# A decoder layer on one core: 66 buffers instead of 51, an RWKV norm without a root, joined softmax steps, and x divided by its rms from piece 20 instead of 35

## The chip, the cores and the metric

The kernel runs on one core of one Trainium2 chip. Five engines work on their own queues: TensorE (PE, with its weight loads shown apart as PEld), VectorE (DVE), ScalarE (ACT), GpSimd (POOL) and SyncE (SP), which here issues nearly all DMAs. The metric is the device time of one execution in microseconds; of several executions the median counts. A profile is one more execution with the profiler on; its span runs from the first to the last instruction of the program.

## The reference

One layer over 256 tokens of width 2048, in float32. Two groups of heads read the same normed x through one projection of 7832 columns:

```python
hn = rms_norm(h, pre_norm_g); proj = hn @ w_in            # 2048 -> 7832
q, kv6, gates, z_a, feat_b, z_b = split(proj)
# group A, 8 query heads on 2 key heads: compressed blocks, selected blocks, window
o = g0 * softmax(q kc + bias) vc + g1 * softmax(q ks + bias) vs + g2 * softmax(q kw + bias) vw
# group B, 16 heads of 64: RWKV-7
kk = k * k_k;  kk = kk / max(sqrt(sum(kk * kk)), 1e-12)   # per head
state = state * w_t + (state a_t) b_t^T + v_t k_t^T;  y = state r_t   # a = -kk, b = kk * a
mix = concat([o * silu(z_a), (groupnorm(y) + bonus) * silu(z_b)])
h = h + rms_norm(mix @ w_out, post_norm_g)
```

## The kernel before

**Pieces.** The projection is worked off in pieces of 128 output columns, in the order of the list `FM`: piece 0 for the two LoRAs, 12 pieces of the first half of RWKV (k, r, v), 8 pieces of compressed, selected and window keys (13 to 20), 12 pieces of RWKV's second half, 8 of q, 16 of z; a token-major part stands after piece 36. Each piece runs over 16 blocks of 128 rows of x, in two half pieces of 8 (`half_piece`). To keep float32 precision every operand is split into a rounded high part and a low rest; a half piece loads one block of weights (512 KB, SP, L312, tile `rf`), ACT rounds it (L320, tile `hf`), DVE subtracts (L321, tile `lf`), and PE multiplies three times: high by high x, high by low x, low by high x. Several blocks are loaded and split ahead of PE. All matmuls come from one helper line, L169; transposes are L198.

**The two forms of a piece.** The high and low part of x lie side by side in `xs_` (tiles xs_75 and xs_76 in the rows below). Up to piece `N_SWITCH - 1` x is not yet divided by its rms, both products with the high weights go into the same 256 columns, and the evacuation multiplies by the reciprocal rms (`evacuate`, L614, one DVE instruction). From piece `N_SWITCH` on (`beside`) x has been divided, and one matmul of 512 columns does both products side by side; then the evacuation adds the two halves, an ACT copy (L616) and a DVE instruction (L617):

```python
if beside:
    mm(pt[:], H[:, k, :], xHL[kk_], start=kk_ == 0, stop=False)
else:
    mm(pt[:, :T], H[:, k, :], xH[kk_], start=kk_ == 0, stop=False)
    mm(pt[:, :T], H[:, k, :], xL[kk_], start=False, stop=False)
```

For the change of form `stage` fetches x a second time, 2 transfers of 1 MB (L524), into 2 times 8 buffers, and multiplies it (16 DVE instructions, L527); it starts 6 pieces ahead of the switch. `renewed` splits it anew into `xs_` (4 ACT copies L537, 4 DVE L538). So that PE has work meanwhile, the two pieces ahead of the switch and the two behind it are done first half by first half, then second half by second half.

**Other work.** RWKV's first half: per 128 columns (`block`, four of them) `k_norm` sums squares per head on PE, `k_rsqrt` takes the root on ACT and the reciprocal on DVE (L686) for two at a time, `rwkv_k` builds scaled keys, `rwkv_r` a masked product (L782). Then `solve` inverts 64 triangular blocks in a loop of 62 DVE instructions (L832, L834), with round trips through DRAM before (`us`, L819 and L825) and after (`zs`, `zt`, L841 to L859), and runs four chunks of the state. The second half does the same later. A group normalisation (L983 to L1002) ends each half. `compress` multiplies 8 blocks of 512 KB (`in_cw`, L1029), fetched by `fetch_cw` when at least 12 buffers are free. `nsa_head`, eight times, does logits, softmax and the weighted sum. Last comes the output projection in 4 groups of 512 columns (tiles `ho`, `lo`); its products with group A's mix (tiles mixA) come first for three groups, the ones with RWKV's mix (mixB) after.

**What sets the order.** The generators are stepped in lanes by a counter of PE time, and a scheduler of the framework with its own timing model then fixes each engine's instruction order at build time. On the chip every engine works off its queue in that order. Temporary storage is one arena of `UNITS` buffers of 1 KB per partition, handed out by `Pool.find`, which weighs how long a buffer has been free.

Of the kernel before, what the change touches and what calls it, by code (L numbers as in the profile page):

```python
# [16 lines left out]
P = 128  # L17
# [36 lines left out]

N_SWITCH = 35

# [5 lines left out]

UNITS = 51
NSMALL = 2912

NLAST = 4
# [15 lines left out]
class Pool:  # L82
# [8 lines left out]
    def find(self, k, step=1):  # L91
        best = None
        for a in range(0, len(self.busy) - k + 1, step):
            if not any(self.busy[a:a + k]):
                beside = (a > 0 and self.busy[a - 1]) + (a + k < len(self.busy) and self.busy[a + k])
                late = max(0.0, max(self.since[a:a + k]) - self.clock[0])
                key = (late, -beside if k < 3 else 0, a if k >= 3 else -a)
                if best is None or key < best[0]:
                    best = (key, a)
        return None if best is None else best[1]  # L100
# [34 lines left out]
def hybrid_block(ctx: ExitStack, tc: tile.TileContext, xT, xtok, wfm, wtm, wout, vecs, gpost, lora, table,  # L135
# [535 lines left out]
    def k_norm(A, i, m):  # L671
        sq = yield from sb()
        ACT.activation(sq[:], A.ks[i], AF.Square, scale=vcol(V_KK, m))
        sp = yield from bank()
        yield from head_sums(sp, sq)
        DVE.tensor_scalar(A.nrm[i], sp[:, :T], 1e-24, None, op0=ALU.max)
        sp.free(2.0)
        yield 0.5

    def k_rsqrt(A, i):  # L680
        nrm = A.pair[i // 2].ap.rearrange("p (a b t) -> p a b t", a=2, b=2)[:, 1]
        yield 1.5
        ACT.activation(nrm, nrm, AF.Sqrt)  # L683
# [20 lines left out]
    def rwkv_k(A, i, m):  # L704
# [3 lines left out]
        for a in range(2):  # L708
# [15 lines left out]
        pi = yield from sb()  # L724
        kk = yield from sb()
        st.prs = pr
# [5 lines left out]
        POOL.tensor_copy(A.PC[:, i, :], pr4[:, :, 63:64].rearrange("p c o -> p (c o)"))  # L732
        DVE.scalar_tensor_tensor(kk[:], k, vcol(V_KK, m), A.nrm[i], op0=ALU.mult, op1=ALU.mult)  # L733
        DVE.tensor_tensor(k, k, fk[:], op=ALU.mult)
# [5 lines left out]
        DVE.tensor_tensor(KB[:, :, 0:4:3, :], k.rearrange("p (a b t) -> p a b t", a=2, b=2), pi4, op=ALU.mult)  # L740
        kk4 = kk.ap.rearrange("p (c t) -> p c t", c=4)
        DVE.tensor_tensor(A.AR[:, i, :, 0, 1:64], kk4[:, :, 1:64], pr4[:, :, 0:63], op=ALU.mult)
        POOL.tensor_copy(A.AR[:, i, :, 0, 0:1], kk4[:, :, 0:1])  # L743
        yield 0.8
        DVE.tensor_tensor(ta[:], ta[:], kk[:], op=ALU.mult)
# [348 lines left out]
    def nsa_head(h, qts):  # L1094
# [52 lines left out]
        yield 1.0  # L1147
        for i in range(2):
            DVE.tensor_scalar(sm[:, i, :], sm[:, i, :], 1e-30, None, op0=ALU.max)
            DVE.reciprocal(sm[:, i, :], sm[:, i, :])  # L1150
            DVE.tensor_tensor(sm[:, i, :], sm[:, i, :], gate[:, i, h:24:8], op=ALU.mult)
            n = (7, 15)[i]
            src = lc[:, i, None, 0:n].to_broadcast([P, 2, n])
            hh_ = lcs[:, i, 0:64].rearrange("p (r n) -> p r n", r=2)[:, :, 0:n]
            DVE.tensor_scalar(hh_, src, sm[:, i, 0:1], None, op0=ALU.mult)
            DVE.scalar_tensor_tensor(lcs[:, i, 64:64 + n], lc[:, i, 0:n], sm[:, i, 0:1],
                                     lcs[:, i, 0:n].bitcast(F32), op0=ALU.mult, op1=ALU.subtract)
            for j in (1, 2):
                dst = parts[i][j][2]
                if i == 1:  # L1160
                    ACT.activation(dst, dst, AF.Copy, scale=sm[:, i, j:j + 1])
                else:
                    DVE.tensor_scalar(dst, dst, sm[:, i, j:j + 1], None, op0=ALU.mult)
            yield 1.2

# [91 lines left out]
    for j, (nm, i) in enumerate(FM):  # L1257
# [13 lines left out]
        elif nm == "k":  # L1271
# [235 lines left out]
```

## Time and profile before

| | |
|---|---|
| median of 3 executions | 559.15 us (558.38 to 561.14) |
| the profiled execution | 558.53 us, of which the span is 556.7 us |
| PE busy, PEld busy | 542.6 us (97%), 492.7 us (88%) |
| DVE, ACT, POOL busy | 434.2 us (78%), 319.5 us (57%), 54.9 us (10%) |
| granted TensorE clock | 0.998 |
| DMA | 102.02 MB, mean 183 GB/s |

A row of a group reads: line, engine, operation, output and inputs by the program's names, count, then busy time, mean duration of one in ns, and the idle time of the engine just before it with what ended it. A row of the timeline reads: start in us from the span's start, length of the run of like instructions, engine and line, what it is, count, and in brackets the idle time before it and its releaser. A busy PE is not a PE at its peak, since the ends of matmuls overlap; the distance between two starts is the better measure.

### The profile page before, as it was taken

The page shows a single profiled execution, that of the slowest core. Times are in us where ns is not written, and L with a number is a line of the kernel's source. Part 1 is how long each engine was busy: PE and PEld are TensorE (multiplying, and loading weights), DVE is VectorE, ACT ScalarE, POOL GpSimd, SP SyncE. Part 2 cuts the span into 40 slices and gives each one's busy share as a digit, 9 for nine tenths or more (in the row PEclk, how much of TensorE's full clock was granted, in tenths as well). Part 3 has the DMA queues.
Part 4 walks back from the last instruction along what each step waited for, and adds up shares of the span by engine and source line. Part 5 has one row for each costly group of instructions (what it writes and reads, how often), then busy time and mean ns, then how long its engine had stood idle before and what let it go on. Part 6 is the DMA issues. An engine that isn't in the chain of part 4 may idle for free.

```text
span 556.7 us, 11510 instructions
## 1 busy us (share of the span) xinstructions
PE 542.6 (97%) x4448; PEld 492.7 (88%) x4448; DVE 434.2 (78%) x910; ACT 319.5 (57%) x592; POOL 54.9 (10%) x93
## 2 busy tenths in 40 slices
PE   9999999998999999999999899999999999899995
PEld 8999999998999999988998788988888887688883
DVE  6888997984998976697799969997856675746654
ACT  6958854644436532545857858765665546455532
POOL 3101310420000000001305100100000000000000
PEclk9999999999999999999999999999999999999999
DMA  8957455477755576553346435445632466456624
GB/s 298 381 195 268 142 172 176 142 249 225 263 193 171 180 203 222 182 172 95 110 150 211 139 108 169 154 161 167 193 127 86 136 219 271 168 189 220 195 79 151
DMA packets 41170, 102.02 MB, mean 183 GB/s; under 512 B 14203, under 2 KB 16412, under 8 KB 40476
## 3 DMA queue, kind: packets, MB, share of 16 engines
q1 hardware_dynamic: 40828, 100.98, 55.1%
q8 instruction: 35, 0.57, 0.4%
q10 hardware_dynamic: 288, 0.31, 0.2%
q14 instruction: 19, 0.16, 0.1%
HBM read 96.03 MB, written 5.24 MB: 182 GB/s over the span
## 4 chain that ended last, share of the span: by engine, by line
PE 84%; DVE 6%; DMA 5%; ACT 2%; issue 1%; SPq 1%; DVEq 0%; ACTq 0%
PE banks L169 82%; DMA arena<-in_cw_dram 2%; PE banks L198 2%; DMA zs<-arena 1%; DMA xr<-in_xT_dram 1%; DMA us<-GR 1%; DMA arena<-zt 1%; DVE GR L782 1%; DVE arena L1002 0%; DVE arena L527 0%; DVE arena L834 0%; DVE arena L832 0%; ACT arena L1142 0%; ACT L987 0%; ACT L715 0%
## 5 line engine op out<-in xcount | busy, mean ns | idle before, releaser
L169 PE MATMUL banks<-arena 128*32 128x128 f32 (+3 forms) x470 | 29.5, 253 | 3.2 <-DMA arena<-in_cw_dram 1.8
L169 PEld LDWEIGHTS banks<-arena 128*32 128x32 f32 (+3 forms) x470 | 25.0, 136 | 7.2 <-DMA arena<-in_cw_dram 2.2
L832 DVE TENSOR_TENSOR arena<-arena 64x31 f32<-64x31 f32 (+15 forms) x62 | 20.4, 329 | 6.2 <-DMA arena<-us 5.6
L631 ACT ACTIVATE small<-small 128x256 f32<-128x256 f32 x25 | 12.3, 501 | 17.6 <-DVE small L614 17.6
L834 DVE TENSOR_TENSOR arena<-arena 64x31 f32<-64x31 f32 (+15 forms) x62 | 20.4, 330 | 0.7
L198 PE MATMUL banks<-small,arena 128*128 128x128 f32 x96 | 15.4, 277 | 1.8 <-DVE arena L989 0.7
L198 PEld LDWEIGHTS banks<-small,arena 128*128 128x128 f32 x96 | 11.1, 140 | 4.2 <-DVE arena L989 1.1
L686 DVE RECIPROCAL arena<-arena 128x256 f32<-128x256 f32 x8 | 13.6, 1730 | 1.3 <-ACT arena L683 1.3
L1142 ACT ACTIVATE arena<-arena,mx 128x128 f32<-128x128 f32 (+1 forms) x32 | 14.1, 443 | 0.0
L632 DVE SCALAR_TENSOR_TENSOR arena<-small 128x256 f32<-128x256 f32 x25 | 11.8, 477 | 2.0 <-ACT small L631 1.9
L719 POOL TENSOR_SCALAR arena<-arena,small 128x256 f32<-128x256 f32 x8 | 9.3, 1164 | 39.3 <-ACT arena L717 39.1
L1138 DVE CUSTOM_DVE_ANT_0 arena<-banks,arena 128x128 f32<-128x128 f32 (+1 forms) x32 | 10.0, 347 | 3.0 <-DMA zt<-arena 3.0
L614 DVE SCALAR_TENSOR_TENSOR small<-banks,small 128x256 f32<-128x256 f32 x29 | 11.9, 417 | 0.1
L169 PEld LDWEIGHTS banks<-VS,GR 128*64 128x64 f32 x256 | 9.6, 137 | 2.5 <-issue 1.4
L955 POOL MEMSET arena<- 64x256 f32 x12 | 3.7, 307 | 81.2 <-DVE lf__2469 L321 44.8
L782 DVE TENSOR_TENSOR GR<-banks,small 128x1024 f32<-128x1024 f32 x8 | 9.7, 1215 | 2.3 <-PE banks L169 2.2
L169 PE MATMUL banks<-VS,GR 128*64 128x64 f32 x256 | 11.4, 228 | 0.0
L743 POOL COPY AR<-arena 128x4 f32<-128x4 f32 x8 | 7.3, 909 | 34.9 <-DVE arena L733 34.9
L169 PE MATMUL banks<-AR,arena 64*128 64x128 f32 x128 | 10.0, 287 | 0.0
L716 POOL TENSOR_SCALAR arena<-arena 128x256 f32<-128x256 f32 x8 | 8.1, 1018 | 17.5 <-ACT arena L715 17.5
L527 DVE SCALAR_TENSOR_TENSOR arena<-arena,small 128x256 f32<-128x256 f32 x16 | 6.5, 479 | 4.3 <-DMA arena<-in_xT_dram 4.3
L169 PEld LDWEIGHTS banks<-AR,arena 64*128 64x128 f32 x128 | 8.1, 187 | 1.4 <-issue 0.3
(1166 smaller groups left out, 1802.4 us busy)
## 6 DMA issues: line engine op xcount, KB each, us to landing
arena<-in_cw_dram SPq DMA_DIRECT2D x8, 512.0 KB, 5.2
arena<-in_wfm_dram SPq DMA_DIRECT2D x4, 512.0 KB, 9.2
arena<-in_xT_dram SPq DMA_DIRECT2D x2, 1024.0 KB, 5.9
xres<-in_xtok_dram SPq DMA_DIRECT2D x2, 1024.0 KB, 5.7
out_dram<-y SPq DMA_DIRECT2D x7, 256.0 KB, 2.4
xr<-in_xT_dram SPq DMA_DIRECT2D x3, 512.0 KB, 7.2
bscr<-arena SPq DMA_DIRECT2D x1, 1536.0 KB, 5.9
arena<-bscr SPq DMA_DIRECT2D x8, 128.0 KB, 2.2
```

The lines of the kernel that those rows point to most:

```text
L169: last[0] = PE.matmul(o, lhsT, rhs, **kw)
L198: PE.transpose(out=o, in_=i, identity=idn)
L614: DVE.scalar_tensor_tensor(o, pt[:, :T], scale, rbc, op0=ALU.mult, op1=ALU.mult)
L631: ACT.activation(tm, f[:, 0:T], AF.Copy, scale=vcol(V_MU, c))
L632: DVE.scalar_tensor_tensor(o, f[:, 1:T + 1], omu[:, c:c + 1], tm, op0=ALU.mult, op1=ALU.add)
L686: pace(DVE.reciprocal(A.nrm[i + j], A.nrm[i + j]))
L719: POOL.tensor_scalar(fk[:], ta[:], ka2[:, m:m + 1], ka1[:, m:m + 1], op0=ALU.mult, op1=ALU.add)
L782: DVE.tensor_tensor(A.GR[:, i].rearrange("p h c t -> p (h c) t"), gp.ap.rearrange("p h (c t) -> p (h c) t", c=4), gmask[:, None, :].to_bro ...
L832: DVE.tensor_tensor(t_, U[:, 0:j, j:j + 1].to_broadcast([64, j, w]), Z[:, j:j + 1, j:32].to_broadcast([64, j, w]), op=ALU.mult)
L834: DVE.tensor_tensor(Z[:, 0:j, j:32], Z[:, 0:j, j:32], t_, op=ALU.add)
L1138: DVE.tensor_tensor_reduce(out=dst, in0=src, in1=bb, scale=1.0, scalar=-3.0e38, op0=ALU.add, op1=ALU.max, accum_out=mx[:, i, j:j + 1])
L1142: ACT.activation(dst, dst, AF.Exp, bias=mx[:, i, j:j + 1], accum_out=sm[:, i, j:j + 1])
```

## The change

Five things at once. The arena has 66 buffers instead of 51 (the room comes from a DMA scratch area set to 1 KB) and its choice adds `REST` = 40 us to the time after which a buffer counts as rested. RWKV's norm takes no root: since the product of two normed vectors is wanted, the reciprocal of the sum of squares is taken from PSUM at once and multiplied in later; `k_rsqrt` and its root on ACT go. The per-head steps after the softmax handle both row blocks with one instruction each. And `N_SWITCH` is 20 instead of 35.

```diff
-N_SWITCH = 35
+N_SWITCH = 20
-UNITS = 51
+UNITS = 66
+REST = 40.0
...
-                late = max(0.0, max(self.since[a:a + k]) - self.clock[0])
+                late = max(0.0, max(self.since[a:a + k]) + REST - self.clock[0])
...
-        DVE.tensor_scalar(A.nrm[i], sp[:, :T], 1e-24, None, op0=ALU.max)
-        sp.free(2.0)
+        DVE.reciprocal(A.nrm[i], sp[:, :T])
+        sp.free(3.0)
         yield 0.5
 
-    def k_rsqrt(A, i):
...
-        ACT.activation(nrm, nrm, AF.Sqrt)
-        yield 1.5
+    def k_ready(A, i):
         for j in range(2):
-            pace(DVE.reciprocal(A.nrm[i + j], A.nrm[i + j]))
+            yield 0.3
             A.normed[i + j] = True
-            yield 1.2
...
-        DVE.scalar_tensor_tensor(kk[:], k, vcol(V_KK, m), A.nrm[i], op0=ALU.mult, op1=ALU.mult)
+        DVE.scalar_tensor_tensor(A.AR[:, i, :, 0, 1:64], k4[:, :, 1:64], vcol(V_KK, m), pr4[:, :, 0:63], op0=ALU.mult,
+                                 op1=ALU.mult)
+        POOL.tensor_scalar(A.AR[:, i, :, 0, 0:1], k4[:, :, 0:1], vcol(V_KK, m), None, op0=ALU.mult)
+        DVE.scalar_tensor_tensor(ta[:], k, vcol(V_KK, m), ta[:], op0=ALU.mult, op1=ALU.mult)
...
-        DVE.tensor_tensor(A.AR[:, i, :, 0, 1:64], kk4[:, :, 1:64], pr4[:, :, 0:63], op=ALU.mult)
-        POOL.tensor_copy(A.AR[:, i, :, 0, 0:1], kk4[:, :, 0:1])
         yield 0.8
-        DVE.tensor_tensor(ta[:], ta[:], kk[:], op=ALU.mult)
+        DVE.scalar_tensor_tensor(ta[:], A.nrm[i], 1e24, ta[:], op0=ALU.min, op1=ALU.mult)
...
+        POOL.memset(lc, 0.0)
...
-        for i in range(2):
-            DVE.tensor_scalar(sm[:, i, :], sm[:, i, :], 1e-30, None, op0=ALU.max)
-            DVE.reciprocal(sm[:, i, :], sm[:, i, :])
-            DVE.tensor_tensor(sm[:, i, :], sm[:, i, :], gate[:, i, h:24:8], op=ALU.mult)
...
+        DVE.tensor_scalar(sm, sm, 1e-30, None, op0=ALU.max)
+        DVE.reciprocal(sm, sm)
+        DVE.tensor_tensor(sm, sm, gate[:, :, h:24:8], op=ALU.mult)
+        lgv = bass.AP(tensor=lg.tensor, offset=lg.offset, ap=[lg.ap[0], [384, 2], [1, 128]])
+        DVE.tensor_tensor(lgv, lgv, sm[:, 0, 1:3, None].to_broadcast([P, 2, P]), op=ALU.mult)
+        for j in (1, 2):
+            dst = parts[1][j][2]
+            ACT.activation(dst, dst, AF.Copy, scale=sm[:, 1, j:j + 1])
+        DVE.tensor_tensor(lc, lc, sm[:, :, 0:1].to_broadcast([P, 2, 16]), op=ALU.mult)
+        DVE.tensor_copy(lcs[:, :, 0:64].rearrange("p i (r n) -> p i r n", r=2)[:, :, :, 0:16],
+                        lc[:, :, None, :].to_broadcast([P, 2, 2, 16]))
+        DVE.tensor_tensor(lcs[:, :, 64:80], lc, lcs[:, :, 0:16].bitcast(F32), op=ALU.subtract)
+        yield 2.4
...
-                rw.append(k_rsqrt(A, i % 4 - 1))
+                rw.append(k_ready(A, i % 4 - 1))
...
-    nc = _bacc.Bacc("TRN2", target_bir_lowering=False, num_devices=1)
+    nc = _bacc.Bacc("TRN2", target_bir_lowering=False, num_devices=1, dynamic_dma_scratch_size=1024)
```

Since the scheduler fixes the order anew, it differs on every engine. Three places are shown; a row is line, operation, output and inputs, size, count, and lines of the changed kernel stand two or three off (L1029 is L1026 there, L321 is L323, L169 is L171, L198 is L200).

SP's queue around the compression weights (`in_cw`, for `compress`), before:

```order
L1035 DMA small<-in_cw_dram 128x256
L312 DMA rf__1420<-in_wfm_dram 128x1024
L312 DMA rf__1471<-in_wfm_dram 128x1024
L312 DMA rf__1518<-in_wfm_dram 128x1024
L312 DMA rf__1560<-in_wfm_dram 128x1024
L312 DMA rf__1603<-in_wfm_dram 128x1024
L1029 DMA arena<-in_cw_dram 128x1024
L312 DMA rf__1647<-in_wfm_dram 128x1024
L1029 DMA arena<-in_cw_dram 128x1024
L312 DMA rf__1684<-in_wfm_dram 128x1024
L312 DMA rf__1724<-in_wfm_dram 128x1024
L1029 DMA arena<-in_cw_dram 128x1024
```

and with the change (rf__1428 is the first half of piece 17, as rf__1420 is before; L526 is the second fetch of x):

```order
L1032 DMA small<-in_cw_dram 128x256
L1026 DMA arena<-in_cw_dram 128x1024 x3
L314 DMA rf__1428<-in_wfm_dram 128x1024
L526 DMA arena<-in_xT_dram 128x2048
L314 DMA rf__1478<-in_wfm_dram 128x1024
L1026 DMA arena<-in_cw_dram 128x1024 x2
L816 DMA us_1459<-GR_675 32x16x32 x3
L314 DMA rf__1521<-in_wfm_dram 128x1024
```

Three of the eight compression weights now go out in one row ahead of piece 17, instead of one by one between pieces 19 and 25, and the second fetch of x stands behind them.

DVE's queue at the multiplication of the refetched x, before (L878 and L892 belong to `solve`, lf__2579 to piece 32):

```order
L321 TENSOR_TENSOR lf__2548<-rf__2546,hf__2549 128x1024
L878 COPY arena<-banks 32x8x32 x4
L527 SCALAR_TENSOR_TENSOR arena<-arena,small 128x256 x8
L321 TENSOR_TENSOR lf__2579<-rf__2577,hf__2580 128x1024
L614 SCALAR_TENSOR_TENSOR small<-banks,small 128x256
```

and with the change (L616 evacuates piece 14, L1040 builds compression blocks, lf__1388 is the second half of piece 16):

```order
L323 TENSOR_TENSOR lf__1349<-rf__1347,hf__1350 128x1024
L616 SCALAR_TENSOR_TENSOR arena<-banks,small 128x256
L529 SCALAR_TENSOR_TENSOR arena<-arena,small 128x256 x8
L1040 TENSOR_TENSOR arena<-arena,small 128x32x15
L323 TENSOR_TENSOR lf__1388<-rf__1386,hf__1389 128x1024
```

The eight multiplications now stand between the low parts of the two halves of piece 16.

PE's queue at the end of RWKV's second half, where the transposes of the group normalisation (128x128) stand among matmuls of the output projection, before:

```order
L169 MATMUL banks<-lo__5632,mixAKCL 128x512 x2
L198 MATMUL banks<-small,arena 128x128 x4
L169 MATMUL banks<-ho__5656,mixAKCL 128x512
L169 MATMUL banks<-ho__5656,mixAL 128x512
L169 MATMUL banks<-ho__5656,mixAKCL 128x512
L169 MATMUL banks<-ho__5656,mixAL 128x512
L198 MATMUL banks<-small,arena 128x128 x4
```

and with the change:

```order
L171 MATMUL banks<-ho__5429,mixAKCH 128x512
L171 MATMUL banks<-ho__5429,mixAL 128x512
L171 MATMUL banks<-lo__5428,mixAKCH 128x512
L200 MATMUL banks<-small,arena 128x128 x8
L171 MATMUL banks<-lo__5428,mixAKCH 128x512
```

Between the last matmuls of `solve` (`arena,AR`, 64x128) and the first transposes stood 40 matmuls of 512 columns and now stand 55; between the last transposes and the first product with mixB stood 74, and now 25.

More of the change, by code (lines that the diff above doesn't have):

```diff
@@ L675, in k_norm @@
         yield from head_sums(sp, sq)
-        DVE.tensor_scalar(A.nrm[i], sp[:, :T], 1e-24, None, op0=ALU.max)
-        sp.free(2.0)
+        DVE.reciprocal(A.nrm[i], sp[:, :T])
+        sp.free(3.0)
         yield 0.5
-    def k_rsqrt(A, i):
-        nrm = A.pair[i // 2].ap.rearrange("p (a b t) -> p a b t", a=2, b=2)[:, 1]
-        yield 1.5
-        ACT.activation(nrm, nrm, AF.Sqrt)
-        yield 1.5
+    def k_ready(A, i):
         for j in range(2):
-            pace(DVE.reciprocal(A.nrm[i + j], A.nrm[i + j]))
+            yield 0.3
             A.normed[i + j] = True
-            yield 1.2
     def begin(hb):
@@ L724, in rwkv_k @@
         pi = yield from sb()
-        kk = yield from sb()
         st.prs = pr
@@ L732, in rwkv_k @@
         POOL.tensor_copy(A.PC[:, i, :], pr4[:, :, 63:64].rearrange("p c o -> p (c o)"))
-        DVE.scalar_tensor_tensor(kk[:], k, vcol(V_KK, m), A.nrm[i], op0=ALU.mult, op1=ALU.mult)
+        k4 = k.rearrange("p (c t) -> p c t", c=4)
+        DVE.scalar_tensor_tensor(A.AR[:, i, :, 0, 1:64], k4[:, :, 1:64], vcol(V_KK, m), pr4[:, :, 0:63], op0=ALU.mult,
+                                 op1=ALU.mult)
+        POOL.tensor_scalar(A.AR[:, i, :, 0, 0:1], k4[:, :, 0:1], vcol(V_KK, m), None, op0=ALU.mult)
+        DVE.scalar_tensor_tensor(ta[:], k, vcol(V_KK, m), ta[:], op0=ALU.mult, op1=ALU.mult)
         DVE.tensor_tensor(k, k, fk[:], op=ALU.mult)
@@ L740, in rwkv_k @@
         DVE.tensor_tensor(KB[:, :, 0:4:3, :], k.rearrange("p (a b t) -> p a b t", a=2, b=2), pi4, op=ALU.mult)
-        kk4 = kk.ap.rearrange("p (c t) -> p c t", c=4)
-        DVE.tensor_tensor(A.AR[:, i, :, 0, 1:64], kk4[:, :, 1:64], pr4[:, :, 0:63], op=ALU.mult)
-        POOL.tensor_copy(A.AR[:, i, :, 0, 0:1], kk4[:, :, 0:1])
         yield 0.8
-        DVE.tensor_tensor(ta[:], ta[:], kk[:], op=ALU.mult)
+        DVE.scalar_tensor_tensor(ta[:], A.nrm[i], 1e24, ta[:], op0=ALU.min, op1=ALU.mult)
         DVE.scalar_tensor_tensor(KB[:, :, 1:3, :], ta.ap.rearrange("p (a b t) -> p a b t", a=2, b=2), -1.0, pi4,
                                  op0=ALU.mult, op1=ALU.mult)
-        for t_ in (ta, kk, pi):
+        for t_ in (ta, pi):
             t_.free(1.0)
@@ L1147, in nsa_head @@
         yield 1.0
-        for i in range(2):
[L1149 to L1164, printed above, removed]
+        DVE.tensor_scalar(sm, sm, 1e-30, None, op0=ALU.max)
[11 more added lines that the diff above has]
+        yield 2.4
         ptp, ctp = yield from bank21()
```

## The prediction

> **What bounds the kernel now.** I read the page's busy times first. PE is the engine to watch:
>
> ```profile
> PE 542.6 (97%) x4448; PEld 492.7 (88%) x4448; DVE 434.2 (78%) x910; ACT 319.5 (57%) x592; POOL 54.9 (10%) x93
> ```
>
> A busy share of 97% does not say that PE works at its pace, so the second view is the timeline of PE, where the distance between starts gives the pace: three rows from a stretch of pieces ahead of the switch, and three from one behind it.
>
> ```profile
> 38.88 2.08 PE L169 MATMUL banks<-xs,hf__475 128*128 128x256 f32 x16
> 40.80 1.12 PE L169 MATMUL banks<-xs,lf__474 128*128 128x256 f32 x8
> 41.76 1.48 PE L169 MATMUL banks<-xs,hf__505 128*128 128x256 f32 x11
> ...
> 348.18 1.99 PE L169 MATMUL banks<-xs,hf__4211 128*128 128x512 f32 x8
> 350.01 1.12 PE L169 MATMUL banks<-xs,lf__4210 128*128 128x256 f32 x8
> 350.96 1.32 PE L169 MATMUL banks<-xs,hf__4256 128*128 128x512 f32 x5
> ```
>
> Ahead of the switch 16 matmuls of 256 columns take 40.80 - 38.88 = 1.92 us and the next 8 take 0.96 us: 120 ns each, 24 to a half piece, 2.88 us. Behind it 8 of 512 columns take 1.83 us (229 ns) and 8 of 256 take 0.95 us (119 ns): 2.78 us a half piece. PE keeps this step through most of the span, so the length of the kernel is PE's list at these steps plus the places where PE waits. Those are the third view, the waits of PE, longest first (us in total, times, longest):
>
> ```profile
> PE banks L169 <- DMA arena<-in_cw_dram: 1.8, 2, 1.5
> PE banks L169 <- ACT arena L1402: 1.1, 1, 1.1
> PE banks L169 <- POOL arena L302: 1.1, 1, 1.1
> PE banks L169 <- DVE arena L1002: 1.0, 1, 1.0
> PE banks L198 <- DVE arena L989: 0.7, 1, 0.7
> PE banks L198 <- DVE arena L1163: 0.6, 1, 0.6
> PE banks L169 <- DMA arena<-zt: 0.6, 1, 0.6
> PE banks L169 <- ACT KT L755: 0.5, 1, 0.5
> PE banks L169 <- DVE lf__3716 L321: 0.5, 1, 0.5
> PE banks L169 <- DVE small L614: 0.5, 1, 0.5
> PE banks L198 <- DVE GR L782: 0.5, 1, 0.5
> ```
>
> L302 is the warm-up at the start and L1402 the finish; neither is touched. The other nine sum to 1.8 + 1.0 + 0.7 + 0.6 + 0.6 + 4 x 0.5 = 6.7 us. That is about all that this change can win beside a shorter list for PE. Last, the windows tell how near DVE, which makes the low parts of the weights, is to its own limit, in two stretches: 60 to 200 us (first half of RWKV, then the loop of `solve`) and 280 to 400 us (second half, heads). Columns are PE, PEld, DVE, ACT and POOL busy, clock, DMA share and GB/s.
>
> ```profile
> 120.00:140.00 20.00, 18.51 (x206) 17.52 (x205) 10.28 (x20) 7.32 (x13) 1.31 (x3) 1.00 0.77 226
> sum 140.00, PE 138.21 PEld 135.03 DVE 120.25 ACT 73.97 POOL 19.31; mean PE 19.74 PEld 19.29 DVE 17.18 ACT 10.57 POOL 2.76
> ```
>
> ```profile
> 300.00:320.00 20.00, 18.01 (x130) 15.30 (x128) 19.98 (x74) 15.52 (x47) 5.14 (x9) 1.00 0.43 144
> sum 120.00, PE 117.25 PEld 104.31 DVE 108.94 ACT 81.60 POOL 12.67; mean PE 19.54 PEld 17.39 DVE 18.16 ACT 13.60 POOL 2.11
> ```
>
> In the first stretch DVE is busy 120.25 of 140 us, and 9.72 of the idle 19.75 lie in one window. In the second it is busy 108.94 of 120, and 19.98 of 20 where four of the nine waits lie.
>
> **The change part by part.** The sum is made against the profiled execution's span, 556.7 us.
>
> *Wide matmuls.* Pieces 20 to 34, 15 pieces or 30 half pieces, change form: 240 matmuls fewer. A half piece goes from 2.88 to 2.78 us, 0.10 x 30 = 3.0 us; by the steps, 2 x 120 - 228 = 12 ns a pair, 240 x 12 = 2.9 us. I take **-2.9**; it lies on PE itself, so nothing hides it. The bounds are 0 and -3.0.
>
> [...]
>
> *Compression weights.* PE waits 1.8 us for `in_cw` because their loads stood single among the others. With 66 buffers three of them leave ahead of piece 17, which is at least two pieces ahead of the place where they left before. **-1.8**, bounds -1.8 and 0.
>
> *Staging x.* Its DVE work moves from where DVE has room into the first stretch:
>
> ```profile
> L527 DVE SCALAR_TENSOR_TENSOR arena<-arena,small 128x256 f32<-128x256 f32 x16 | 6.5, 479 | 4.3 <-DMA arena<-in_xT_dram 4.3
> L538 DVE TENSOR_TENSOR xs<-arena,xs 128x1024 fp32r<-128x1024 f32 x4 | 4.7, 1215 | 0.0
> L616 ACT ACTIVATE small<-banks 128x256 f32<-128x256 f32 x22 | 8.3, 376 | 1.2 <-PE banks L169 0.9
> ```
>
> 6.5 + 4.7 = 11.2 us come into a stretch with 19.75 us idle. ACT's extra copies, 15 x 0.376 = 5.6 us, lie beside PE's work, since ACT is busy 57% of the span; uncovered they would cost that 0.38 us at each bank's release. The DMA is the danger. At its old place DVE stood still for it:
>
> ```profile
> 213.71 3.26 DVE L527 SCALAR_TENSOR_TENSOR arena<-arena,small 128x256 f32<-128x256 f32 x8 [4.28 <-DMA arena<-in_xT_dram]
> ```
>
> Behind that row waited the low part lf__2579 and an evacuation, and of DVE's 4.28 us idle 0.5 us reached PE (the row of L614 in the waits). That 0.5 goes: **-0.5**. At the new place the fetch stands on SP's queue behind three transfers of 512 KB and one block of weights, so it lands no earlier relative to DVE, and a DVE with less room passes more on. Queued behind it on DVE are a compression block and the low parts of pieces 16 and 17, for which PE waits next. I take **+1.5**, a third of 4.28; bounds 0 (it has landed in time) and +4.3 (all of it reaches PE).
>
> *Norm without a root.* The pass L676 goes and the other DVE instructions of the block are exchanged one for one; on ACT the four roots go, each with a table load here and one to go back:
>
> ```profile
> L676 DVE TENSOR_SCALAR arena<-banks 128x256 f32<-128x256 f32 x8 | 3.3, 414 | 0.3 <-PE banks L169 0.2
> L683 ACT ACT_TABLE_LOAD x4 | 5.1, 1283 | 0.1
> ```
>
> DVE saves 8 x 0.414 = 3.3 us, ACT 8 x 1.283 = 10.3 us of loads. All of that lies beside PE's list. Its worth is taken with the next part.
>
> *Joined head steps.* The rows of what goes, and a 256-element product as the measure of what comes:
>
> ```profile
> L1149 DVE TENSOR_SCALAR sm<-sm 128x3 f32<-128x3 f32 x16 | 2.5, 156 | 0.5 <-ACT arena L1142 0.5
> L1150 DVE RECIPROCAL sm<-sm 128x3 f32<-128x3 f32 x16 | 2.6, 163 | 0.1
> L1151 DVE TENSOR_TENSOR sm<-sm,small 128x3 f32<-128x3 f32 x16 | 2.4, 151 | 0.0
> L1155 DVE TENSOR_SCALAR lcs<-lc,sm 128x14 fp32r<-128x14 f32 (+1 forms) x16 | 4.3, 271 | 0.1
> L1156 DVE SCALAR_TENSOR_TENSOR lcs<-lc,sm,lcs 128x7 fp32r<-128x7 f32 (+1 forms) x16 | 3.4, 213 | 0.1
> L1163 DVE TENSOR_SCALAR arena<-arena,sm 128x128 f32<-128x128 f32 x16 | 4.3, 306 | 0.0
> L745 DVE TENSOR_TENSOR arena<-arena 128x256 f32<-128x256 f32 x8 | 3.4, 431 | 0.0
> ```
>
> The first six groups sum to 2.5 + 2.6 + 2.4 + 4.3 + 3.4 + 4.3 = 19.5 us. In their place stand, per head, three instructions on 6 elements (0.16 us each), one product of 256 (0.43) and three small ones (0.27 at most): 1.7 us, 13.7 in all. DVE saves some 6 us here and 1.7 with RWKV's second half, so 108.94 falls to about 101 of 120 us. The waits that a full DVE causes there are L1163 0.6, lf__3716 0.5, L782 0.5 and KT 0.5 (this by way of ACT), 2.1 us. I take half, **-1.1**: a fuller DVE in a newly made order seldom loses every wait. Bounds -2.1 and +1.
>
> *The end of RWKV.* PE waits for the group normalisation:
>
> ```profile
> 463.17 0.66 PE L169 MATMUL banks<-arena,AR 128*64 128x128 f32 x8
> ...
> 473.95 0.66 PE L198 MATMUL banks<-small,arena 128*128 128x128 f32 x4 [0.66 <-DVE arena L989]
> ...
> 477.21 0.50 PE L169 MATMUL banks<-ho__5591,mixAKCH 128*128 128x512 f32 x1 [0.97 <-DVE arena L1002]
> ...
> 494.40 1.07 PE L169 MATMUL banks<-ho__5760,mixB 128*128 128x512 f32 x4
> ```
>
> From the end of the last `solve` matmuls (463.17 + 0.66 = 463.8) to the transposes pass 10.1 us, filled with 40 matmuls (40 x 0.228 = 9.1 us) and a wait; L1002 then holds the next group up. Now 55 matmuls, 12.5 us, stand there, more than 10.1. **-1.6** (0.66 + 0.97); bounds -1.6 and the third rival below.
>
> *Oldest-first buffers* change which write waits for which read; no row of the waits names such a wait beyond those counted, so 0, with 0.6 either way (the wait for `zt`, which keeps its place).
>
> Sum: -2.9 - 1.8 - 0.5 + 1.5 - 1.1 - 1.6 = -6.4 us: span 550.3. What lies around the span is 558.53 - 556.7 = 1.8 us, so 552.1 for a profiled execution; the median of the runs shown is 0.6 above its profiled one. **Predicted: 552.7 us**, own range 549.5 to 556.
>
> **The rivals.**
>
> *All waits go.* With the nine waits and no new one: 556.7 - 2.9 - 6.7 = 547.1, a median of 549.5; 548 with some of the shorter waits that I left out. For it: DVE gets 3.3 + 6 us less work. Against it: the staging moves to the fuller stretch.
>
> *The waits only move.* DVE can't use the idle 9.72 us of the window 120 to 140, where it waits for the round trip before `solve`. Then 11.2 us meet 10.0 us of room and a fetch of 4.28: 1.2 + 4.3 = 5.5 in place of 1.5, and the half of the head waits stays: 552.7 + 4.0 + 1.1 = 557.8, no change that counts. For it speaks that two of DVE's queue rows with L527 stand ahead of low parts; against it that from 140 to 200 DVE was over nine tenths busy while PE hardly waited.
>
> *The wide matmuls bring nothing.* Were a step of PE set by its columns alone, two of 256 would take what one of 512 takes, the term of 2.9 would fall away and 552.7 become 555.6. Against it stand the six rows of steps; for it only that they come from two different stretches. [...]
>
> *Slower: the chain of RWKV's second half sets the end.* The cushion between transposes and mixB shrinks from 74 to 25 matmuls, since `solve` ends later in PE's list. From its last matmul PE still has 12.5 us, 8 transposes (0.9), 25 x 0.228 = 5.7 and the 62.3 us from 494.40 to the end: 81.4 us that nothing shortens. My span of 550.3 puts that last matmul at 468.9, against 463.8 before. Every microsecond by which the staging in DVE delays the loop of `solve`, and that the second half, is paid in full once PE runs out of other work. From 475.3 the gain is gone, from 478.1 the kernel is slower by 0.5%; at 481, 12 us late, it takes 565. For it: DVE's stretch; against it: 12 us is more than everything moved there.
>
> **How the numbers follow.** Forecast 0.43, all waits go 0.14, wide matmuls bring nothing 0.04, waits only move 0.21, slower 0.18. A measurement of this kernel can tell 0.5%, 2.8 us, from no change: faster means under 556.4, slower over 561.9. Faster 0.43 + 0.14 + 0.04 = 0.61, same 0.21, slower 0.18. The range leaves a tenth at either end: 547.5 to 562.
>
> **What would show it.** In the profile of the changed kernel: half pieces from 20 on at 2.78 us; no PE wait for `in_cw`; DVE idle for in_xT at the first multiplication row and a PE wait of 1 to 2 us for a low part near 110 to 125 us; DVE busy near 101 of 120 us among the heads; last `arena,AR` matmuls at about 469 us and no PE wait for L986 or L999. A half piece of 512 columns at 2.88 us, a PE wait of over 4 us near the staging, or last `solve` matmuls after 475 us would make the prediction wrong.

## The result and the profile after

The changed kernel takes **552.42 us** (median of 4 executions, 551.37 to 553.26) against 559.72 us of the kernel before, measured beside it. The ratio is **0.9877, 95% interval 0.9851 to 0.9902** (the two medians alone divide to 0.987). The forecast was 552.7, so the total came out as predicted. How it came about did not, and most of what follows is on that.

The profiled execution has a span of 551.2 us (forecast 550.3). First the busy times on the page of the profile after, then its waits of PE (us in total, times, longest), all of them:

```profile
PE 541.9 (98%) x4208; PEld 483.8 (88%) x4208; DVE 427.4 (78%) x862; ACT 312.2 (57%) x595; POOL 55.7 (10%) x101
```

```profile
PE banks L171 <- DVE arena L1061: 1.8, 1, 1.8
PE banks L171 <- ACT arena L1396: 1.1, 1, 1.1
PE banks L171 <- POOL arena L304: 1.1, 1, 1.1
PE banks L171 <- ACT hf__273 L322: 0.6, 1, 0.6
PE banks L171 <- ACT KT L752: 0.2, 1, 0.2
```

L304 and L1396 are the start and the finish, as before. Of the nine waits of before (6.7 us) only that for KT is left, with 0.2. Two are new: 0.6 near 20 us (ACT does another row first) and 1.8 for the copy L1061, which takes the result of a compression's matmuls out of PSUM. The timeline of PE around a half piece, that wait and the end of RWKV's second half:

```profile
124.44 0.41 PE L171 MATMUL banks<-small,arena 128*128 128x32 f32 x2 [1.78 <-DVE arena L1061]
124.69 3.02 PE L171 MATMUL banks<-xs,hf__1431 128*128 128x256 f32 x13
...
181.65 2.00 PE L171 MATMUL banks<-xs,hf__2124 128*128 128x512 f32 x8
183.49 1.12 PE L171 MATMUL banks<-xs,lf__2123 128*128 128x256 f32 x8
184.45 2.00 PE L171 MATMUL banks<-xs,hf__2152 128*128 128x512 f32 x8
...
468.82 0.66 PE L171 MATMUL banks<-arena,AR 128*64 128x128 f32 x8
```

A half piece now takes 184.45 - 181.65 = 2.80 us. The second row carries something that the waits don't list: 13 matmuls of 256 columns take 2.82 us up to the next start (127.51), 217 ns each in place of 120. The windows show why (PE, PEld, DVE, ACT and POOL busy, then the granted clock, DMA share and GB/s):

```profile
122.00:124.00 2.00, 0.67 (x6) 0.46 (x4) 0.01 (x1) 0.45 (x1) 0.00 (x0) 1.00 0.95 262
124.00:126.00 2.00, 1.56 (x8) 1.56 (x9) 1.80 (x9) 0.00 (x0) 0.00 (x0) 0.70 0.98 393
126.00:128.00 2.00, 2.00 (x12) 2.00 (x11) 2.00 (x6) 0.25 (x1) 0.00 (x0) 0.50 1.01 410
128.00:130.00 2.00, 2.00 (x18) 2.00 (x18) 1.97 (x4) 0.92 (x2) 0.00 (x0) 0.94 0.88 301
```

Right behind the wait PE's clock falls to half for 3.4 us (0.50 from 124.8 to 128.2), which costs 1.56 x 0.30 + 2.00 x 0.50 + 2.00 x 0.06 = 1.6 us more. DVE's timeline tells where the wait comes from:

```profile
111.78 3.26 DVE L529 SCALAR_TENSOR_TENSOR arena<-arena,small 128x256 f32<-128x256 f32 x8 [0.80 <-DMA arena<-in_xT_dram]
...
123.99 0.20 DVE L829 TENSOR_TENSOR arena<-arena 64x31 f32<-64x31 f32 x1 [3.39 <-DMA arena<-us]
124.12 0.27 DVE L1061 COPY arena<-banks 128x128 f32<-128x128 f32 x1
```

DVE waits 0.80 us for the refetched x, and no PE wait follows from it. What holds PE up is the next DMA wait: the first row of `solve`'s loop waits 3.39 us for the round trip of `us`, and the copy that PE needs stands behind it.

**One account for all kernels.** A span is split into PE's waits (the sum of that view, start and finish included), the clock loss (PE's busy time times 1 - clock, over stretches of 2 us from 10 to 536 us), and the rest, which is PE's list at its pace. Span, waits, clock and rest are those of one profiled execution, while the ratio rests on all executions of a kernel. So a row can be off by its execution: those of e_heads and e_root are the slowest of seven (551.75 us against a median of 549.53, and 557.15 against 555.64), that of h_csb18 is the fastest of six (551.74 against 553.31).

| kernel | ratio (95%) | span | waits | clock | rest | loop of `solve`, first and second half, starts |
|---|---|---|---|---|---|---|
| before | 1 | 556.7 | 9.7 | 0.0 | 547.0 | 136.5, 384.8 |
| changed | 0.9877 (0.9851-0.9902) | 551.2 | 4.8 | 1.6 | 544.8 | 124.0, 388.6 |
| e_n20only: piece 20 alone | 1.0172 (1.0139-1.0206) | 568.5 | 17.1 | 7.5 | 543.9 | 146.0, 393.3 |
| e_n35: without piece 20 | 1.0013 (0.9988-1.0037) | 557.7 | 7.1 | 1.7 | 548.9 | 121.9, 384.5 |
| e_u51: without rule and number | 1.0132 (1.0104-1.0160) | 564.5 | 15.9 | 4.6 | 544.0 | 130.3, 396.8 |
| e_rest0: without the rule | 1.0121 (1.0096-1.0147) | 565.4 | 17.7 | 5.6 | 542.1 | 131.0, 400.3 |
| e_u51old: without the number | 0.9929 (0.9905-0.9953) | 554.1 | 7.7 | 1.7 | 544.7 | 122.1, 370.8 |
| e_root: with the root | 0.9928 (0.9896-0.9960) | 555.3 | 8.1 | 3.3 | 543.9 | 128.6, 390.4 |
| e_heads: head steps unjoined | 0.9808 (0.9775-0.9842) | 549.6 | 5.7 | 0.0 | 543.9 | 124.3, 390.9 |
| e_csbact: L1061 on ACT | 0.9866 (0.9836-0.9896) | 549.4 | 3.9 | 0.0 | 545.5 | 123.0, 386.8 |
| h_csb: e_heads and e_csbact | 0.9829 (0.9805-0.9853) | 548.5 | 5.6 | 0.0 | 542.9 | 125.0, 389.8 |
| h_csb18: h_csb, piece 18 | 0.9899 (0.9871-0.9926) | 549.9 | 6.5 | 0.0 | 543.4 | 136.4, 383.2 |
| e_rest30: REST 30 | 0.9853 (0.9833-0.9874) | 548.7 | 6.2 | 0.0 | 542.5 | 123.4, 376.7 |
| e_rest80: REST 80 | 0.9846 (0.9825-0.9867) | 548.8 | 4.9 | 0.0 | 543.9 | 123.7, 369.9 |

The rest goes by the length of PE's list: 547.0 and 548.9 with 4448 matmul instructions, 542.1 to 545.5 (mean 543.8) with 4208; h_csb18 has 4176. That is the wide matmuls' gain, and it is there in every kernel that has them. What else sets these spans apart is waits and lost clock.

### The profile page after: what moved, and what is told of

Read it like the earlier page. It is cut to its first block, busy times and chain, and to the rows that moved or that the text cites. A ratio compares the mean times of both kernels' runs of the same rounds, so it can differ in the third digit from the quotient of the medians.

```text
span 551.2 us, 10942 instructions
## 1 busy us (share of the span) xinstructions
PE 541.9 (98%) x4208; PEld 483.8 (88%) x4208; DVE 427.4 (78%) x862; ACT 312.2 (57%) x595; POOL 55.7 (10%) x101
## 4 chain that ended last, share of the span: by engine, by line
PE 88%; DMA 5%; ACT 2%; DVE 2%; SPq 1%; issue 1%; POOL 0%; DVEq 0%; ACTq 0%
PE banks L171 86%; PE banks L200 2%; DMA xr<-in_xT_dram 1%; DMA arena<-us 1%; DMA us<-GR 1%; DMA rf__3422<-in_wfm_dram 1%; DMA rf__95<-in_wfm_dram 1%; SPq L816 1%; ACT xs L397 0%; POOL arena L713 0%; ACT arena L499 0%; DVE arena L999 0%; ACT L712 0%; DVE GR L779 0%; DVE arena L733 0%
## 5 line engine op out<-in xcount | busy, mean ns | idle before, releaser
L171 PE MATMUL banks<-arena 128*32 128x128 f32 (+3 forms) x470 | 30.2, 253 | 1.1 <-POOL arena L304 1.1
L171 PEld LDWEIGHTS banks<-arena 128*32 128x32 f32 (+3 forms) x470 | 25.7, 136 | 4.5 <-POOL arena L304 1.1
L829 DVE TENSOR_TENSOR arena<-arena 64x31 f32<-64x31 f32 (+15 forms) x62 | 20.4, 329 | 5.2 <-DMA arena<-us 4.5
L618 ACT ACTIVATE small<-banks 128x256 f32<-128x256 f32 x37 | 13.9, 375 | 4.4 <-PE banks L171 4.3
L200 PE MATMUL banks<-small,arena 128*128 128x128 f32 x96 | 14.7, 274 | 0.0
L678 DVE RECIPROCAL arena<-banks 128x256 f32<-128x256 f32 x8 | 13.8, 1740 | 0.8 <-PE banks L171 0.8
L171 PE MATMUL banks<-VS,GR 128*64 128x64 f32 x256 | 13.6, 228 | 0.0
L171 PEld LDWEIGHTS banks<-VS,GR 128*64 128x64 f32 x256 | 10.9, 137 | 1.5 <-issue 0.4
L713 POOL TENSOR_SCALAR arena<-arena 128x256 f32<-128x256 f32 x8 | 9.5, 1189 | 26.1 <-ACT arena L712 26.1
L200 PEld LDWEIGHTS banks<-small,arena 128*128 128x128 f32 x96 | 11.2, 140 | 1.0
L926 DVE COPY VS<-banks 64x512 f32<-64x512 f32 x8 | 5.5, 687 | 7.5 <-PE banks L171 7.5
L956 POOL TENSOR_TENSOR arena<-arena,PC 128x256 f32<-128x256 f32 x4 | 3.3, 836 | 78.7 <-DVE arena L946 49.7
L732 POOL TENSOR_SCALAR AR<-arena,small 128x4 f32<-128x4 f32 x8 | 7.4, 932 | 31.8 <-DVE arena L634 31.8
L171 PE MATMUL banks<-AR,arena 64*128 64x128 f32 x128 | 9.3, 285 | 0.0
L171 PEld LDWEIGHTS banks<-AR,arena 64*128 64x128 f32 x128 | 7.8, 187 | 1.5 <-issue 0.7
```

Source lines behind the costliest of these rows:

```text
L171: last[0] = PE.matmul(o, lhsT, rhs, **kw)
L200: PE.transpose(out=o, in_=i, identity=idn)
L618: ACT.activation(t, pt[:, T:2 * T], AF.Copy, scale=scale)
L678: DVE.reciprocal(A.nrm[i], sp[:, :T])
L713: POOL.tensor_scalar(u[:], u[:], 1.0, None, op0=ALU.add)
L829: DVE.tensor_tensor(t_, U[:, 0:j, j:j + 1].to_broadcast([64, j, w]), Z[:, j:j + 1, j:32].to_broadcast([64, j, w]), op=ALU.mult)
```

## The experiments

None of the experiments changes what is computed.

**Whose are the new wait and the slow clock.** The copy goes to ACT (e_csbact), which is busy for 0.45 of the 4 us from 122 to 126 in the windows above:

```diff
-        DVE.tensor_copy(csb[:, 0:P], cps[:, 0:P])
+        ACT.activation(csb[:, 0:P], cps[:, 0:P], AF.Copy)
```

> The changed kernel (span 551.2 us), but the copy L1061 behind each compression runs on ACT instead of DVE, so it no longer stands behind L829, which waits 3.39 us for the round trip of us. Theory A (the 1.8 us wait for L1061 is the whole of the new loss, and the half clock at 124 to 128 us, some 1.9 us, is its consequence): both go, span 547.5, ratio to before 0.981. Theory B (the low parts behind L829 on DVE are late anyway): PE waits 1 to 1.8 us for a low part in its place, span 550 to 551.2, ratio 0.986 to 0.988. Theory C (the half clock has nothing to do with the wait): the wait goes and the clock is still lower in some windows, span 549.4, ratio 0.9845.

Measured: span 549.4, ratio 0.9866. The new rows among its waits, and the place itself in PE's timeline:

```profile
PE banks L171 <- DVE xs L540: 0.5, 1, 0.5
PE banks L171 <- issue: 0.3, 1, 0.3
```

```profile
122.66 0.31 PE L171 MATMUL banks<-small,arena 128*128 128x32 f32 x2
122.80 1.80 PE L171 MATMUL banks<-xs,hf__1431 128*128 128x256 f32 x13
```

The wait is gone, the 13 matmuls take 1.64 us to the next start (124.44), and no stretch between start and finish is under full clock. So in these two profiles both losses hang on this one copy. The clock is not lost every time, though: of the changed kernel's own four executions three had a mean clock of 0.994 to 0.996 and spans of 550.1 to 551.5, and one had 0.999 and 549.6 (3.4 us at half rate take some 0.003 off the mean, an estimate). The profiled span gained 1.8 us, not 3.7, since 0.8 us of smaller waits came a little later and the rest is 0.7 higher, and between the medians (551.32 and 552.42, ratios 0.9866 and 0.9877) no gain can be told. The span is the one that theory C gave, but C expected the clock to stay low; the cause is as in A, the size is not.

**Without the piece-20 switch**, the rest kept (e_n35, `N_SWITCH = 35`):

> The changed kernel with the switch back at piece 35 (N_SWITCH 35), everything else kept. Half pieces 20 to 34 take 2.88 us again, +2.9 us. Theory A (the new wait for L1061 and the half clock come from the early compression weights and the round trip of us, which keep their order): they stay, the old wait of 0.5 us for L614 comes back, span 551.2 + 3.4 = 554.6, ratio to before 0.994. Theory B (they come from the refetched x, which now goes back to its old place): wait and half clock go, -3.7, span 550.9, ratio 0.987.

Measured 1.0013, span 557.7, 3 us more than theory A said: nothing is left of the gain. The waits' first two rows:

```profile
PE banks L171 <- DVE arena L1061: 2.0, 1, 2.0
PE banks L171 <- DVE xs L540: 1.9, 2, 1.4
```

The wait for L1061 stays (2.0) although no x is refetched near it, so theory B falls: here too L1061 stands behind L829, which waits 3.74 us for `us`. This wait cost no clock; the kernel lost 1.7 us of clock at 404 us instead. The old staging place costs 1.9. The switch is worth 6.5 us of span here: some 4 in the rest, 2.3 in waits.

**Without the arena's part.** e_u51 takes back number and rule, e_rest0 the rule alone (`REST = 0.0`), e_u51old the number alone (`UNITS = 51`):

> The changed kernel with the arena of before: 51 buffers, the old choice among them. In the order the compression weights leave one or two at a time again, and the copy L1061 no longer stands right behind L829 on DVE. Theory A (the early loads removed the wait for in_cw and made the new one): a PE wait for in_cw of 1 to 1.8 us is back, the wait for L1061 and the half clock (1.8 + 1.9) are gone, span 549 to 550, ratio to before 0.984. Theory B (the arena is what removed the waits and the new one is owed to the refetched x): in_cw back with 1.8 and a wait for a low part behind L829 of 1 to 2, the other waits of before partly back, span 553 to 555, ratio 0.991 to 0.995.

> The changed kernel with 66 buffers but the old choice among them (REST 0). In the order the compression weights leave as late and as singly as with 51 buffers. Theory A (what matters of the arena is only that these loads leave early, and that takes both the number and the oldest-first choice): as with 51 buffers, in_cw 1 to 1.8 back and the wait for L1061 gone, span 549 to 550.5, ratio 0.984 to 0.986. Theory B (the number of buffers alone matters): as the changed kernel, 551 within 0.6, ratio 0.988.

> The changed kernel with 51 buffers but the oldest-first choice (REST 40) kept. Theory A (the rule is what counts, the number only lets the weights leave early): the waits for VS and for evacuations that the old choice brought (10 us) stay away, span 551 to 554, ratio to before 0.988 to 0.992. Theory B (the rule needs the spare buffers to have old ones to choose from): as with the old choice, span 560 to 566, ratio 1.005 to 1.015.

Measured 564.5, 565.4 and 554.1. The first two expectations were wrong by 9 us and more under either theory; in e_u51 `in_cw` is not even among the waits. The third is theory A's, just outside its range. The longest waits of e_rest0, then pieces of its PE timeline:

```profile
PE banks L171 <- DVE VS L926: 5.0, 4, 2.5
PE banks L171 <- DVE arena L619: 3.4, 2, 2.4
PE banks L171 <- DVE small L616: 2.0, 1, 2.0
```

```profile
64.80 3.68 PE L171 MATMUL banks<-xs,hf__751 128*128 128x256 f32 x16 [1.99 <-DVE small L616]
...
441.45 0.73 PE L171 MATMUL banks<-arena 64*64 64x64 f32 x16 [0.53 <-ACT arena L916]
444.64 1.12 PE L171 MATMUL banks<-VS,KT 128*64 128x64 f32 x16 [2.46 <-DVE VS L926]
...
448.11 1.12 PE L171 MATMUL banks<-arena,AR 128*64 128x128 f32 x8
449.70 1.06 PE L171 MATMUL banks<-arena 64*64 64x64 f32 x16 [0.47 <-ACT arena L916]
451.62 0.69 PE L171 MATMUL banks<-VS,KT 128*64 128x64 f32 x16 [0.86 <-DVE VS L926]
...
457.74 2.12 PE L171 MATMUL banks<-xs,hf__5095 128*128 128x512 f32 x8
```

The last three of the four chunks of the second half follow one another with nothing between them, PE waits at the hand-overs, and from 444.6 to 450 it runs at half clock as well (16 matmuls of 64 columns in 1.12 us in place of 0.69). In the changed kernel these three lie between 431 and 469 us with pieces and the output projection among them. PE is not out of other work in e_rest0: four half pieces and the output projection still stand behind the chunks, from 457.7 on. The order, fixed at build time, put them there. The chunks are not all of it either. Waits for evacuations (L616, L619) come to 7.2 us, and two of them, at 64.8 and 320.8, are each followed by a slow stretch that costs another 1.5. How early the two orders part shows on DVE (rows of the changed kernel with -, of e_rest0 with +; lf__268 to lf__276 are low parts in the order in which PE needs them, L502 is side work whose results go to arena buffers):

```
-L502 TENSOR_TENSOR arena<-arena 128x512 x2
-L400 SCALAR_TENSOR_TENSOR xs_76<-xr,small,xs_76 128x256
-L502 TENSOR_TENSOR arena<-arena 128x512
 L323 TENSOR_TENSOR lf__268<-arena,hf__269 128x1024
...
 L323 TENSOR_TENSOR lf__272<-arena,hf__273 128x1024
 L323 TENSOR_TENSOR lf__276<-arena,hf__277 128x1024
+L502 TENSOR_TENSOR arena<-arena 128x512
```

With the old choice the first L502 stands behind three low parts instead of ahead of them, and `solve` then starts 7 us later in the first half (131.0 against 124.0) and 12 us later in the second. That the one leads to the other is likely, but not shown. In all three kernels with the old choice and piece 20 (e_rest0, e_u51, e_n20only) the second loop starts after 393 us, in all others before 391. With 51 buffers the rule does most of it: 554.1 against 564.5. The 2.9 us by which e_u51old is behind the changed kernel are in its waits:

```profile
PE banks L171 <- DVE xs L540: 2.0, 1, 2.0
PE banks L171 <- DVE arena L616: 1.7, 1, 1.7
PE banks L171 <- ACT arena L1396: 1.1, 1, 1.1
PE banks L171 <- DMA arena<-in_cw_dram: 1.1, 1, 1.1
```

`in_cw` is back with 1.1, as the forecast would have it. But the number of buffers does not settle it: e_u51 has 51 and no such wait, e_root has 66 and waits 0.6 us for `in_cw`, h_csb18 has 66 and waits 1.4. The longest wait here, L540, is for the split of the refetched x at the new staging place, and a slow stretch of 1.7 us follows it. What the rule brings, the forecast had put at nothing.

**Is it the rule, or any turn of the order?** REST 30 and 80 in place of 40 give the same instructions in other orders (some 700 lines of difference in PE's list):

> The changed kernel with REST 30 in place of 40: the same instructions and buffers, only which free buffers count as old enough differs a little. Theory A (the rule works by keeping a write from waiting for a recent reader; 30 us is still long against a wait of a few us): span 551.2 within 1, ratio to before 0.986 to 0.989. Theory B (the order that the scheduler makes is what counts, and any turn of it moves the waits): 3 us or more from 551.2, ratio under 0.983 or over 0.993.

> The changed kernel with REST 80 in place of 40, as before the same work. Theory A: span 551.2 within 1, ratio to before 0.986 to 0.989. Theory B: 3 us or more from it, not in the same direction as with 30 of necessity.

Measured 548.7 and 548.8, ratios 0.9853 and 0.9846: outside A's 1 us, inside B's 3. So the rule, from somewhere between 0 and 30 us on, is worth 14 to 17 us with 66 buffers and 10 with 51. (The two kernels without it are not independent draws: the wait of 1.99 us near 65 us is in both.) A mere turn of the order moves the span by some 2.5 us, through rows like these of e_rest30's waits:

```profile
PE banks L171 <- DVE arena L619: 1.9, 1, 1.9
...
PE banks L171 <- DVE arena L1061: 1.0, 1, 1.0
```

The wait for L1061 is 1.8 in the changed kernel and 1.0 here, and here no clock is lost. A difference of 0.3% between two orders says nothing about a part; h_csb18 below shows that 0.7% can come about in this way.

**The norm, and the head steps.** e_root restores `k_rsqrt` with its root and L676's pass, e_heads the per-block loop after the softmax, each in the changed kernel:

> The changed kernel with the norm of RWKV's blocks by root again (L676's pass, the roots on ACT with their table loads, the product by kk as before). Theory A (a sum of parts: the root's 3.3 us on DVE and 10.3 us on ACT lie beside PE, only a part of the old waits near 300 us and at the end of RWKV comes back): span 551 to 553, ratio to before 0.987 to 0.991. Theory B (every part has its worth only in an order that all of them make together, as with the arena's rule, whose undoing alone cost 14 us): the order made anew brings back waits of 4 to 12 us in places that have nothing to do with the root, span 555 to 563, ratio 0.995 to 1.01.

> The changed kernel with the head steps unjoined again (some 6 us more for DVE between 280 and 400 us). Theory A (sum of parts): the waits of a full DVE among the heads come back by half to wholly, 1.1 to 2.1 us, span 552 to 553.5, ratio to before 0.989 to 0.992. Theory B (the order made anew decides): waits of 4 us and more elsewhere, span over 555, ratio over 0.995.

The root costs 4.1 us between the profiled spans and 0.5% between the ratios (0.9928 and 0.9877), whose intervals just overlap. With the pass and the roots in each block `solve` starts at 128.6 instead of 124.0. PE's longest wait stands there; its row, and DVE's,

```profile
129.78 1.08 PE L171 MATMUL banks<-arena 128*32 128x128 f32 x32 [2.08 <-issue]
```

```profile
128.62 0.20 DVE L834 TENSOR_TENSOR arena<-arena 64x31 f32<-64x31 f32 x1 [4.33 <-DMA arena<-us]
128.74 0.94 DVE L1045 TENSOR_TENSOR arena<-arena,small 128x480 f32<-128x480 f32 x1
```

The trace names no releaser ("issue"); PE goes on 0.1 us after L1045 ends, which builds blocks for the compression and stood behind the wait for `us`. Whether it was this row that PE needed is not shown. A slow stretch of twice the length follows (3.3 us). A further wait of 1.7 is for the first half's group normalisation at 285.6. The ratio is just above theory A's, the span at the lower end of theory B's, and the way is B's: no wait of before near 300 us came back. A cost of this size is within what an order made anew can draw, so it is not shown to be the root's own.

For the joined head steps no gain is seen: without them this kernel is faster, 0.9808 (span 549.6 us). The windows of 280 to 400 us, first of the changed kernel and then of e_heads:

```profile
280.00:400.00 120.00, 119.83 (x799) 107.73 (x798) 105.90 (x340) 85.75 (x222) 11.94 (x29) 1.00 0.52 163
```

```profile
280.00:400.00 120.00, 119.90 (x805) 107.01 (x804) 108.25 (x369) 82.47 (x214) 11.76 (x22) 1.00 0.50 163
```

DVE is as busy in e_heads as it was before the change (108.94), and PE still has no wait there among those listed. What e_heads gains lies elsewhere: its wait for L1061 is 0.8 and loses no clock, though its waits in all are 5.7 us against 4.8.

**Piece 20 alone**, in the kernel before (e_n20only, `N_SWITCH = 20`):

> The kernel before with the switch at piece 20 alone (N_SWITCH 20; 51 buffers, the old choice, root and unjoined head steps as before). Theory A (the sum of the forecast: 2.9 us for the wide matmuls, 0.5 for the old wait, 1.5 lost at the new staging): span 556.7 - 1.9 = 554.8, ratio to before 0.9966. Theory B (the staging in the fuller stretch needs the room that the other parts make; without it the order falls apart as it did without the arena's rule): span 560 to 566, ratio 1.005 to 1.017.

Measured 568.5, ratio 1.0172: theory B, and more than it said. The longest waits:

```profile
PE banks L169 <- DMA arena<-in_cw_dram: 3.2, 2, 2.9
PE banks L169 <- DVE VS L929: 2.6, 3, 0.9
PE banks L169 <- DVE arena L946: 2.1, 1, 2.1
```

Here the rest is 543.9, so the matmuls got shorter as computed, but `solve` starts at 146.0 instead of 136.5, some of its chunks stand bare in both halves (231 to 237 us, 246 to 252, 447 to 459), and waits and clock rise from 9.7 to 24.6 us.

**A faster one?** Both finds together (h_csb), and with piece 18:

> The changed kernel with the head steps unjoined and the copy L1061 on ACT. Theory A (the gain of the run with unjoined heads came from the smaller wait and the missing half clock near 124 us, so most of it is the same gain that the copy on ACT brings): span 548 to 550, ratio to before 0.979 to 0.984, no wait for L1061, no window under full clock. Theory B (unjoined heads are worth 3 us by themselves, far from that place): both gains add, span 545.5 to 547, ratio 0.974 to 0.977.

> As the run before (unjoined heads, copy L1061 on ACT), with the switch at piece 18: 4 half pieces more in the wide form. Theory A (PE's list shortens by 4 x 0.1 us and the waits stay): 0.4 us under the run before, ratio lower by 0.0007, not to be told apart. Theory B (every order made anew draws its waits anew): 2 us or more from it in either direction, and other rows among the waits.

h_csb: 0.9829 and 548.5 us, the numbers of A, and no wait for L1061. A wait of like length, for which the trace names no releaser, stands 5 us later:

```profile
129.89 0.41 PE L171 MATMUL banks<-arena 128*32 128x128 f32 x4 [1.87 <-issue]
```

That A has the cause is not shown: the copy on ACT alone had gained 0.1%, the unjoined heads alone 0.7%. h_csb18: 0.9899, slower by 0.7% for 4 wider half pieces, with 1.4 us for `in_cw` back among its waits: theory B. The fastest is e_heads at 549.53 us (0.9808); its interval and the changed kernel's do not overlap, but it is one draw of an order.

## Why the prediction was right in its sum, and where it was wrong

- *Wide matmuls, -2.9*: right. Half pieces of 2.80 us in place of 2.88, 2.4 us over 30 of them, and a rest that is lower by 2.2 in the changed kernel and by 4.1 between the means, where the kernels with 4208 scatter over 3.4. The rival that they bring nothing falls. By these half pieces a joined pair saves 10 ns: 0.08 us for 8 pairs.
- *Compression weights, -1.8*: the wait went, as forecast. That the number of buffers removed it is not shown: at 51, with the rule kept, 1.1 is back, but e_u51 has none at 51, and two kernels with 66 have 0.6 and 1.4.
- *Staging, -0.5 and +1.5*: the old wait went. At the new place it was not the refetched x that PE paid for (DVE waited 0.80, PE nothing) but the round trip of `us`, by way of L1061: 1.8 and 1.6 of clock, 3.4 in all. The wait came at 124.4, inside the stretch that I had named, and the cost lies inside the bounds of 0 and 4.3, but by another cause: I had named a low part, and the wait for L1061 stays with the switch at 35. In e_u51old the refetched x does cost at the new place, 2.0 us by way of its split.
- *Norm and head steps, -1.1 at the heads*: the waits there fell by 1.9 us, but not because DVE has less to do. I had taken half on the ground that a fuller DVE seldom loses every wait; that was an estimate of mine which no run shows, and here 0.2 of the 2.1 was left. DVE stood at 105.9 of 120, not 101, and at 108.25 (e_heads) they are gone too. (Of the four waits that I put beside the full window of 300 to 320 us, the one for L782 lies just behind it, at 320.1.) With the root back the kernel is 0.5% slower, by waits outside the heads, where I gave the norm nothing of its own; one order more does not show that the root is the cause.
- *End of RWKV, -1.6*: right. Last `arena,AR` at 468.8 + 0.66 = 469.5, forecast 468.9; no wait for the normalisation.
- *Oldest-first buffers, 0 with 0.6 either way*: **this step failed.** I argued that no row of the waits names such a wait. The rows of before can't: the waits that came without the rule belong to an order that before did not have. The staging of x is not all that calls them up, since the one at 64.8 us in e_rest0 comes 44 us ahead of the refetch. Measured 14 us for the rule (e_rest0) and 2.9 for the number (e_u51old), the latter near what a mere turn of the order moves.
- *New and not in the sum*: the clock, 1.6.

Put together: list -2.2 (the profiled rest), waits -4.9, clock +1.6, span -5.5. The forecast had -2.9 and -3.5, and no clock. The five edits as a whole did remove most of what before showed. That the total came so close is in part luck: the new place cost 1.9 us more than forecast and the start 0.6, while waits that I had left standing or halved fell by 2.2 more (0.8 at the heads, 0.6 for `zt`, 0.8 of short ones). As worths of single edits the terms are wrong: taken out one at a time the edits are worth 6.5 (switch), 13.3 (arena), 4.1 (norm) and -1.6 (heads), 22.3 in all against 5.5. The first two are beyond what a turn of the order does, the last two are not. What one edit is worth depends on the others. Piece 20 alone is 1.7% slower, the other edits without it bring nothing. *The waits only move* describes e_n20only and e_n35 better than the changed kernel. The slower rival's mechanism, a late chain in the second half and PE without other work, is not what the slow kernels show, though it looks alike: their chunks are bare from 441 (e_rest0) and 447 us (e_n20only), end by 459, ahead of the 475 that I named, and PE has work left that the order put behind them.

What stays open: whether the rule works on the chip through fewer waits on recent readers, or only through the order that the scheduler derives from them. No run held the order fixed while it changed the buffers. Nor is it settled why the changed kernel is 0.7% slower than the one with unjoined head steps; between the profiles e_heads gains 1.6 us of clock and 0.9 of rest and loses 0.9 in waits, and its profiled execution is the slowest of its seven.

## What to carry to other kernels

Where a scheduler fixes the order anew, split each span into the list, the waits and the clock loss: here the list's part was forecast well from steps (-2.9, and -2.2 in the profiled rest), the waits' part belonged to all edits together (one at a time they were worth 22.3 us, as a whole 5.5), and the row-by-row sum over edits said nothing of one alone. A worth of one edit that is smaller than the scatter between orders, here up to 0.7%, is not known from one order. Look at how a change moves the start of the longest side chain; here the choice among free buffers alone moved it by 7 and 12 us. And DVE's wait of 3.39 us for the DMA of `us` held up what stood behind it in the queue, a copy of 0.27 us included for which PE waited 1.78 us; moving that copy took the wait away, but the medians (551.32 and 552.42) show no gain.

## What the runs showed of the hardware

In seven of the 14 profiled executions the granted clock fell to 0.50 for a while between 10 and 536 us. In the changed kernel this came right behind a single PE wait of 1.78 us and cost a further 1.6 us; in e_rest0 it came with a wait of 2.46 us and others following, and cost 2.6. But the wait of 2.05 us in e_n35 cost nothing. Of the 16 PE waits of 1.6 us and more in the 14 profiled executions, ten have a slow stretch within 3 us behind them, and six have none. Nor did every slow stretch follow a wait: e_n35 lost 1.7 us at 404 us without any listed wait, behind 4 us of small matmuls (32 and 64 columns on part of the array):

```profile
403.74 1.08 PE L171 MATMUL banks<-arena 32*32 32x32 f32 x44
404.74 3.20 PE L171 MATMUL banks<-xs,hf__4943 128*128 128x512 f32 x7
407.78 1.10 PE L171 MATMUL banks<-xs,lf__4942 128*128 128x256 f32 x8
```

7 matmuls of 512 columns take 3.04 us, 434 ns each in place of 228. The seven kernels that lost clock have nine slow stretches that cost 1.5 to 1.7 us each and four that cost 2.6 to 3.3. By the windows each of the nine lasts 3.4 us and each of the four 6.8. The loss need not come in every execution: three of the changed kernel's four had a mean clock of 0.994 to 0.996, one had 0.999. Why a stretch at half clock followed the wait of 1.78 us and none that of 2.05 is not shown.
